# Loading tokens and weights of the first projection one k tile at a time, in a two-layer decoder trunk on Trainium2

## Chip, cores and metric

The kernel runs on one core of a Trainium2 chip. The metric is the device time of one execution in microseconds (us); the times shown are medians of several runs. The engines are TensorE (PE in the profile: matrix products; PEld is its weight load), VectorE (DVE), ScalarE (ACT), GpSimd (POOL) and SyncE (SP), which here issues every data transfer.

## What is computed

Two layers of a hybrid causal decoder run over 592 token columns: 16 learned meta tokens, 64 sample tokens (8 sequences of 8) and 512 prompt tokens, with a model width of 1024. Only the start of layer 0 matters here:

```python
xn = rms_norm(x, norm_mix[0])        # y = x * rsqrt(mean(x*x) + EPS) * gain
z  = xn @ w_in_ab[0]                 # q, k, v, o, input and forget gates; then q, k, v, gate
# heads 0..3: mLSTM, heads 4..7: retention; output projection; ConvFFN; layer 1 (HGRN2); ConvFFN; final norm
```

The norm's root is one number per token, so the kernel multiplies the tokens by the gain alone, projects them, and applies the root to the result of the projection. The sum of squares over the 1024 features is needed for that, but not for the products.

## The kernel before

Tokens lie with features on partitions, in eight k tiles of 128 features by 592 tokens (`x[0]` to `x[7]`). For float32 accuracy each operand of a product is split in two parts of a reduced format: a high part (a cast on ACT, line 295 for weights, line 215 for tokens) and a low part (what the cast lost, a subtraction on DVE, line 299 and line 216). Each product is then three: high by high, and the two mixed ones.

A block of the projection is one stretch of output columns. Block 0 and block 1 (`token_proj`) give the values of two mLSTM heads each, and four columns of gates: 260 output columns. Tokens are the stationary operand there, in five token tiles (one of 80 tokens, four of 128). Block 0 runs k by k over token tiles 0 to 3 at once, then does `norm_rows` (the sums of squares, `ssp`, by products with a column of 1/1024, then the root `rt` by small DVE operations), then tile 4. Block 1 runs tile by tile, and after tile 1 does `norm_bcast`, which spreads the root over partitions (`rb`). Block 2 is an action, `setup`, that loads constants. Then come the projections of q, k and so on (`proj`), eight k tiles of 128 columns each.

A block's weights are loaded by `raw_weights` into tiles `wr` (two buffers), each for four k tiles and 260 columns: one transfer of 256 columns (512 KB) and one of 4 columns (8 KB). `Split.make` turns one into `wh` and `wl` (three buffers each). A transfer into a `wr` buffer waits until the former one has been split. `stream` fetches the loads of two splits ahead of the running block.

`start` loads `x[0]` and the vectors, makes the gained tokens of k tile 0 (`gained`: `h` and `xl`) and its square (`norm_square`). Then block 0's weights are loaded, and `go_on` does the same for k tiles 1 to 7. Squares of tiles 1, 3 and 5 and their sum are made on POOL as a second partial sum, those of the others by ACT (square) and DVE (sum). Line 1600 adds the two partial sums; `norm_rows` makes products of both.

The row stream (`rows`, gates of the mLSTM heads) is interleaved later by the clock of products that the builder keeps. It writes into `mgr`, a tile that `setup` first fills with zeros: line 982 multiplies the constant tile `ca` by zero on POOL. All transfers go through SP in order.

The framework orders each engine's instructions when the program is built, by priority (program order) and by its own plan of what is ready; on the chip each engine then runs its list in order.

Of the kernel before, what the change touches and what calls it, by code (L numbers as in the profile page):

```python
# [9 lines left out]
F32 = mybir.dt.float32  # L10
F32R = mybir.dt.float32r
# [3 lines left out]
ALU = mybir.AluOpType  # L15
PSUM = bass.MemoryType.PSUM

D = 1024
# [5 lines left out]
NT = NMETA + NSAM + NP  # L24
# [13 lines left out]
V_NMIX, V_NFFN, V_NFIN, V_GNA, V_GNB, V_GNH, V_LB, V_CB, V_CW = 0, 16, 32, 40, 44, 48, 56, 72, 116  # L38
# [61 lines left out]
def trunk_kernel(ctx: ExitStack, tc: tile.TileContext, I, O):  # L100
    nc = tc.nc
    V, S, G, T = nc.vector, nc.scalar, nc.gpsimd, nc.tensor
    ld, st_q = nc.sync, nc.sync
# [3 lines left out]
    wp = ctx.enter_context(tc.tile_pool(name="wp", bufs=1))  # L107
# [54 lines left out]
    def tmp(name, n=NT, dt=F32):  # L162
        return tp.tile([128, n], dt, name=name, tag="t", bufs=4)
# [28 lines left out]
    vec = cp.tile([128, 248], F32, name="vec")  # L192
    gnh = cp.tile([128, 16], F32, name="gnh")
    csm = cp.tile([128, 165], F32, name="csm")
# [3 lines left out]
    ones = cp.tile([128, 128], F32R, name="ones")  # L198
    mean = cp.tile([128, 1], F32, name="mean")
# [4 lines left out]
    x = [None] * 8  # L204
    state = {"x": "xa", "h": "xb", "ssq": {}}

    def xslot(c, name, dt=F32):
        return ap.tile([128, NT], dt, name=f"{name}{c}", tag=f"{state[name]}{c}")

    def gained(c, gain):  # L210

        hi = xslot(c, "h", F32R)
        lo = ap.tile([128, NT], F32R, name=f"xl{c}", tag=f"xl{c}")
        g = vec[:, gain + c:gain + c + 1]
        S.activation(hi, x[c], AF.Copy, scale=g)
        V.scalar_tensor_tensor(out=lo, in0=x[c], scalar=g, in1=hi.bitcast(F32), op0=ALU.mult, op1=ALU.subtract)
        state[c] = (hi, lo)

    def norm_square(c, a=0, b=NT, eng=V, part=0):

        sq = tmp("sq" if part in state["ssq"] else "ssq")
        if eng is V:
            S.activation(sq[:, a:b], x[c][:, a:b], AF.Square)
        else:
            eng.tensor_tensor(out=sq[:, a:b], in0=x[c][:, a:b], in1=x[c][:, a:b], op=ALU.mult)
        if part not in state["ssq"]:
            state["ssq"][part] = sq
        else:
            acc = state["ssq"][part][:, a:b]
            eng.tensor_tensor(out=acc, in0=acc, in1=sq[:, a:b], op=ALU.add)  # L230
# [48 lines left out]


    class Split:
        def __init__(self, k, n, src, sums=None):
            self.k, self.n, self.src, self.sums, self.made = k, n, src, sums, None
            line.append(self)

        def sum_up(self):
# [4 lines left out]
        def make(self):  # L291
            self.sum_up()
            src = self.src() if callable(self.src) else self.src
            hi = wp.tile([128, self.k, self.n], F32R, name="wh", tag="wh", bufs=3)
            S.copy(hi, src)  # L295
            if line:
                line[0].sum_up()
            lo = wp.tile([128, self.k, self.n], F32R, name="wl", tag="wl", bufs=3)
            V.tensor_tensor(out=lo, in0=src, in1=hi.bitcast(F32), op=ALU.subtract)  # L299
            self.made = (hi, lo)  # L300
# [51 lines left out]
    def weights(*views):  # L352

        return [Split(r.shape[1], r.shape[2], r) for r in map(raw_weights, views)]

    def got(ws):
        return [sp.get() for sp in ws]
# [46 lines left out]
    def cols(w, c0, n=128):  # L404
        return w.rearrange("(k p) n -> p k n", p=128)[:, :, c0:c0 + n]
# [8 lines left out]
            post(p[:, off + first:off + NT])  # L414
        return (lambda: weights([cols(w, c0)]), body)

    def token_proj(w, pieces, emit, first=False, hook=None):

        n = sum(b for _, b in pieces)

        def load():
            return weights(*[[cols(w, c0, b)[:, k0:k0 + 4, :] for c0, b in pieces] for k0 in (0, 4)])

        def products(out, halves, k, t0, r):
            hi, lo = halves[k // 4]
            xh, xl = state[k]
            for i, (a, b) in enumerate(((xh, hi), (xh, lo), (xl, hi))):
                matmul(out, lhsT=a[:, t0:t0 + r], rhs=b[:, k % 4, :], start=(k == 0 and i == 0),
                       stop=(k == 7 and i == 2))

        def body(halves):
            p, halves = None, got(halves)
            if first:

                ps = [mm("tp"), mm("tp"), px("tq")]
                outs = [(t, r, ps[t // 2][:, 512 * (t % 2):512 * (t % 2) + 512]) for t, (t0, r) in enumerate(TILES)]
                for ts in ((0, 1, 2, 3), (4,)):
                    for k in range(8):
                        for t in ts:
                            t0, r = TILES[t]  # L440
                            products(outs[t][2][:r, 0:n], halves, k, t0, r)
                        yield
                    if ts[0] == 0:
                        norm_rows()
                for o in outs:
                    emit(*o)
                return
            for t, (t0, r) in enumerate(TILES):
                if hook is not None and t in (0, 1, 4):
                    p, o = px("tq"), 0  # L450
                else:
                    o = 512 * (t % 2)
                    p = mm("tp") if t % 2 == 0 else p
                for k in range(8):
                    products(p[:r, o:o + n], halves, k, t0, r)
                    yield
                emit(t, r, p[:, o:o + 512])
                if hook is not None and t == 1:
                    hook()
        return (load, body)  # L460
# [497 lines left out]
    def layer0():  # L958
        w = I["w_in_ab"][0]
        ca = ap.tile([128, 1776], F32, name="ca", tag="u1")  # L960
# [5 lines left out]
        mgr = ap.tile([36, 2, 5, 128], F32R, name="mgr", tag="u2")  # L966
# [8 lines left out]
        def setup():  # L975
            ld.dma_start(out=ca[:, 0:1600], in_=I["c_ab"])
            sel = tmp("sel", 512)[0:36, :]
            ld.dma_start(out=sel, in_=I["c_sel"])
            ld.dma_start(out=rm4, in_=I["c_rm"][0:4, :])
            ld.dma_start(out=gb, in_=I["gate0"])  # L980
            S.copy(selr, sel)
            G.tensor_scalar(out=mgr.rearrange("p a t i -> p (a t i)"), in0=ca[0:36, 0:1280], scalar1=0.0, scalar2=None,
                            op0=ALU.mult)
            for t in range(5):
                o = 4 * min(t, 1)
                G.tensor_copy(epst[:, :, t], epsr[:, o:o + 4])
            G.memset(tok3[64:128, 0, :, :], 1.0)
            V.tensor_scalar(out=gnh, in0=vec[:, V_GNA:V_GNA + 16], scalar1=0.5, scalar2=None, op0=ALU.mult)

        def emit_va(hp):  # L990
            f0 = emit_v(f"a{hp}")

            def f(t, r, p):
                f0(t, r, p)
                if t == 0:
                    if hp == 0:
                        G.memset(gt, 0.0)
                    G.memset(vs[f"a{hp}"][:, :, :, 128:129], 1.0)
                S.activation(gt[:r, t, 32 * hp:32 * hp + 4], p[:r, 256:260], AF.Copy, scale=state["rt"][:r, t:t + 1])
            return f  # L1000
# [222 lines left out]
        def mixer_b(h):  # L1223
# [54 lines left out]
            for t, (t0, r) in enumerate(TILES[1:]):  # L1278
# [10 lines left out]
        kb = lambda h: proj(w, 2568 + 128 * h, post_rot(h, 128 ** -0.5, "bl", "k"))  # L1289
        g_ = lambda h: proj(w, 3592 + 128 * h, silu_gate(("b", h)))  # L1290
        vb = lambda hp: token_proj(w, [(3080 + 256 * hp, 256)], emit_v(f"b{hp}"))
        blocks = [token_proj(w, [(1024, 256), (2048, 4)], emit_va(0), first=True),
                  token_proj(w, [(1280, 256), (2052, 4)], emit_va(1), hook=norm_bcast), action(setup),
                  q_(0), k_(0), q_(1), k_(1), o_(0), q_(2), k_(2), o_(1), q_(3), k_(3), o_(2), vb(0),
                  qb(0), kb(0), o_(3), qb(1), kb(1), g_(0), vb(1), qb(2), kb(2), g_(1), qb(3), kb(3), g_(2), g_(3)]
# [285 lines left out]

    xin = I["x0"].rearrange("p c n -> c p n")

    def start():
        for c in range(8):
            x[c] = xslot(c, "x")
        V.memset(ones.bitcast(F32), 1.0)
        V.memset(mean, 1.0 / D)
        ld.dma_start(out=x[0], in_=xin[0])
        ld.dma_start(out=vec, in_=I["vectors"])  # L1590
        gained(0, V_NMIX)
        norm_square(0)

    def go_on():
        for c in range(1, 8):
            ld.dma_start(out=x[c], in_=xin[c])
            gained(c, V_NMIX)
            norm_square(c, 0, NT, *((G, 1) if c in (1, 3, 5) else (V, 0)))
        both = state["ssq"]
        V.tensor_tensor(out=both[0], in0=both[0], in1=both.pop(1), op=ALU.add)  # L1600
        ld.dma_start(out=csm, in_=I["c_small"])


    SPANS = ((NMETA, TILES[3][0]), (TILES[3][0], NT))
# [29 lines left out]
                                       op1=ALU.mult)  # L1634
            ld.dma_start(out=O["y"][:, c:c + 2, a - NMETA:b - NMETA], in_=y)

    start()
    b0, s0, mix0 = layer0()
    b1, s1, mix1 = layer1()
    blocks = b0 + mix_proj(I["w_out_ab"][0], mix0, 0, V_NFFN, xin)  # L1640
# [2 lines left out]
    blocks.append(action(spill))  # L1643
    blocks += b1 + mix_proj(I["w_out_c"][0], mix1, 14, V_NFFN + 8, xd)
    blocks += ffn(1, None, SPANS)
    first = blocks[0][0]()
    go_on()
    blocks[0] = (lambda: first, blocks[0][1])
    interleave(stream(blocks), s0 + s1 + [finish(*sp) for sp in SPANS], 2)


# [57 lines left out]
```

## Time and profile before

| what | value |
|---|---|
| median of 3 runs | 1589.66 us (1588.35 to 1589.88) |
| profiled execution, its own time | 1593.28 us |
| its span, first to last instruction | 1591.4 us |
| mean granted PE clock in it | 0.989 of full speed |
| PE busy | 1537.6 us |
| DVE, ACT, POOL busy | 1153.5, 729.0, 208.3 us |

The profile is of one execution; times in it count from the span's start. A row of the timeline gives the start, the duration, the engine, the line, the operation and its tiles (out<-in), how many were merged, and in brackets how long the engine had been idle before and what ended that. A matmul's duration reaches into the next one's, so the distance of their starts is the pace. A window's row gives the busy time and the count of instructions of each engine, then the granted clock, the share of the DMA engines and GB/s. Granted clock 1.00 is 2.4 GHz and 0.50 is 1.2 GHz.

### The profile page before, as it was taken

How to read it: one execution, taken by the hardware profiler on the slowest of the kernel's cores; microseconds unless marked ns; L12 is line 12 of the kernel's file. 1: busy time of each engine (PE TensorE's matmuls, PEld its weight loads, DVE VectorE, ACT ScalarE, POOL GpSimd, SP SyncE). 2: the span in 40 equal slices, each digit the busy share in tenths (PEclk: the TensorE clock that was granted, in tenths of full speed). 3: DMA queues.
4: the chain of work that ended last, by engine and by line, in shares of the span. 5: the costliest groups of instructions: out<-in, count | busy, mean ns of one | idle time of the engine just before them, and what ended most of it. 6: DMA issues, size and time to landing. Idle time of an engine off the chain costs nothing. (4 is left out here: it accounts for less than half of the span.)

```text
span 1591.4 us, 32114 instructions
## 1 busy us (share of the span) xinstructions
PE 1537.6 (97%) x13100; PEld 1489.0 (94%) x13100; DVE 1153.5 (72%) x2351; ACT 729.0 (46%) x1316; POOL 208.3 (13%) x402
## 2 busy tenths in 40 slices
PE   5999999999999999999999899999999999999996
PEld 5999998999999999999999798998999999999995
DVE  6576564658987887777646776766689888788875
ACT  3543343325454444444445566464454444444453
POOL 4000000000120001011003524333002000000001
PEclk9999999999999999999999999999999999999998
DMA  6555646233223323223522231223332232333234
GB/s 165 102 81 113 86 90 78 80 123 107 80 67 96 91 80 94 80 82 119 159 80 59 65 96 65 88 91 104 93 103 80 80 94 82 92 93 94 67 108 130
DMA packets 217620, 148.57 MB, mean 93 GB/s; under 512 B 7512, under 2 KB 208984, under 8 KB 217472
## 3 DMA queue, kind: packets, MB, share of 16 engines
q1 hardware_dynamic: 217472, 146.51, 34.4%
q8 instruction: 103, 1.69, 0.4%
q14 instruction: 45, 0.37, 0.1%
HBM read 131.84 MB, written 14.65 MB: 92 GB/s over the span
## 5 line engine op out<-in xcount | busy, mean ns | idle before, releaser
L295 ACT CAST wh<-wr 128x1024 fp32r<-128x1024 f32 (+3 forms) x240 | 232.7, 970 | 403.2 <-PE dp L123 121.6
L299 DVE TENSOR_TENSOR wl<-wr,wh 128x1024 fp32r<-128x1024 f32 (+3 forms) x240 | 271.4, 1131 | 75.8 <-ACT wh L295 73.8
L123 PE MATMUL dp<-h,wh 128*128 128x296 f32 (+1 forms) x1088 | 242.3, 304 | 0.7 <-ACT v_c L918 0.5
L123 PE MATMUL dp<-h,wl 128*128 128x296 f32 (+1 forms) x1088 | 236.7, 298 | 0.0
L123 PE MATMUL dp<-xl,wh 128*128 128x296 f32 (+1 forms) x1088 | 236.6, 298 | 0.0
L123 PE MATMUL dp<-bh,wh 128*128 128x296 f32 (+2 forms) x864 | 188.4, 299 | 0.8 <-DVE x L491 0.4
L123 PE MATMUL dp<-bh,wl 128*128 128x296 f32 (+2 forms) x864 | 186.4, 297 | 0.0
L123 PE MATMUL dp<-bl,wh 128*128 128x296 f32 (+2 forms) x864 | 186.4, 297 | 0.0
L123 PEld LDWEIGHTS dp<-h,wh 128*128 128x128 f32 x1088 | 174.9, 189 | 4.3 <-issue 1.8
L123 PEld LDWEIGHTS dp<-h,wl 128*128 128x128 f32 x1088 | 176.4, 189 | 0.0
L123 PEld LDWEIGHTS dp<-xl,wh 128*128 128x128 f32 x1088 | 176.2, 189 | 0.0
L123 PEld LDWEIGHTS dp<-bh,wh 128*128 128x128 f32 x864 | 139.0, 188 | 3.1 <-issue 1.4
L123 PEld LDWEIGHTS dp<-bl,wh 128*128 128x128 f32 x864 | 139.5, 188 | 0.0
L123 PEld LDWEIGHTS dp<-bh,wl 128*128 128x128 f32 x864 | 139.2, 188 | 0.0
L123 PE MATMUL ac<-h,wh 128*128 128x296 f32 (+1 forms) x408 | 123.8, 303 | 3.0 <-DVE cs L704 2.7
L123 PE MATMUL ac<-h,wl 128*128 128x296 f32 (+1 forms) x408 | 121.5, 298 | 0.0
L123 PE MATMUL ac<-xl,wh 128*128 128x296 f32 (+1 forms) x408 | 121.1, 297 | 0.0
L123 PE MATMUL tp<-wh,h 128*128 128x256 f32 (+3 forms) x280 | 85.1, 305 | 14.8 <-ACT wh L295 11.2
L595 ACT ACTIVATE cv<-cv 128x612 f32<-128x612 f32 (+1 forms) x44 | 31.1, 708 | 117.0 <-DVE cv L591 117.0
L295 ACT CAST wh<-s 128x1024 fp32r<-128x1024 f32 x68 | 56.8, 836 | 60.7 <-PE sb L123 34.6
L123 PEld LDWEIGHTS ac<-h,wh 128*128 128x128 f32 x408 | 76.9, 188 | 6.9 <-DVE cs L704 5.6
L123 PE MATMUL tp<-wl,h 128*128 128x256 f32 (+3 forms) x280 | 81.7, 292 | 0.3 <-DVE wl L299 0.3
(477 smaller groups left out, 3455.9 us busy)
## 6 DMA issues: line engine op xcount, KB each, us to landing
wr<-in_w_ffn_in SPq DMA_DIRECT2D x88, 512.0 KB, 3.8
wr<-in_w_in_ab SPq DMA_DIRECT2D x32, 512.0 KB, 7.6
wr<-in_w_ffn_out SPq DMA_DIRECT2D x32, 512.0 KB, 3.4
wr<-in_w_in_c SPq DMA_DIRECT2D x32, 512.0 KB, 3.9
wr<-in_w_ffn_out SPq DMA_DIRECT2D x24, 384.0 KB, 3.5
x<-in_x SPq DMA_DIRECT2D x16, 296.0 KB, 5.2
out_H<-s_s SPq DMA_DIRECT2D x8, 576.0 KB, 2.8
wr<-in_w_out_ab SPq DMA_DIRECT2D x16, 256.0 KB, 2.7
```

What stands on the lines that cost most here:

```text
L123: T.matmul(out, lhsT=lhsT, rhs=rhs, **kw)
L295: S.copy(hi, src)
L299: V.tensor_tensor(out=lo, in0=src, in1=hi.bitcast(F32), op=ALU.subtract)
L595: S.activation(env_["cv"][:, b0:612], env_["cv"][:, b0:612], AF.Silu)
```

## The change

`start` becomes a function of the k tile, which the first block's load calls for each of the eight in turn. It loads `x[k]`, then the weights of that k tile (one transfer of 256 columns, 128 KB, and one of 4 columns, 2 KB), and then emits the gain and the square of that tile. The vectors are loaded ahead of `x[0]`, and the small constants `csm` after the last k tile, as before. The weights are split one k tile at a time (`single`): eight casts and eight subtractions of 260 columns in place of two and two of 1040. All squares are made on ACT and all sums on DVE, in one partial sum, so the merge at line 1600 and five of ten `ssp` products go. `mgr` is filled in three pieces of up to 512 columns from `rb` in place of one of 1280 from `ca`.

```diff
     class Split:
-        def __init__(self, k, n, src, sums=None):
+        def __init__(self, k, n, src, sums=None, single=False):
...
             hi = wp.tile([128, self.k, self.n], F32R, name="wh", tag="wh", bufs=3)
+            if self.single:
+                lo = wp.tile([128, self.k, self.n], F32R, name="wl", tag="wl", bufs=3)
+                for k in range(self.k):
+                    S.copy(hi[:, k, :], src[:, k, :])
+                    V.tensor_tensor(out=lo[:, k, :], in0=src[:, k, :], in1=hi[:, k, :].bitcast(F32), op=ALU.subtract)
+                self.made = (hi, lo)
+                return
...
         def load():
+            if chunks is not None:
+                raws = [wp.tile([128, 4, n], F32, name="wr", tag="wr", bufs=2) for _ in range(2)]
+
+                def one(k):
+                    o = 0
+                    for c0, b in pieces:
+                        ld.dma_start(out=raws[k // 4][:, k % 4, o:o + b], in_=cols(w, c0, b)[:, k, :])
+                        o += b
+
+                for k in range(8):
+                    chunks(k, one)
+                return [Split(4, n, r, single=True) for r in raws]
...
-            G.tensor_scalar(out=mgr.rearrange("p a t i -> p (a t i)"), in0=ca[0:36, 0:1280], scalar1=0.0, scalar2=None,
-                            op0=ALU.mult)
+            for a in range(0, 1280, 512):
+                b = min(a + 512, 1280)
+                G.tensor_scalar(out=mgr.rearrange("p a t i -> p (a t i)")[:, a:b], in0=state["rb"][0:36, 0:b - a],
+                                scalar1=0.0, scalar2=None, op0=ALU.mult)
...
-        blocks = [token_proj(w, [(1024, 256), (2048, 4)], emit_va(0), first=True),
+        blocks = [token_proj(w, [(1024, 256), (2048, 4)], emit_va(0), first=True, chunks=start),
...
-    def start():
-        for c in range(8):
-            x[c] = xslot(c, "x")
-        V.memset(ones.bitcast(F32), 1.0)
-        V.memset(mean, 1.0 / D)
-        ld.dma_start(out=x[0], in_=xin[0])
-        ld.dma_start(out=vec, in_=I["vectors"])
-        gained(0, V_NMIX)
-        norm_square(0)
-
-    def go_on():
-        for c in range(1, 8):
-            ld.dma_start(out=x[c], in_=xin[c])
-            gained(c, V_NMIX)
-            norm_square(c, 0, NT, *((G, 1) if c in (1, 3, 5) else (V, 0)))
-        both = state["ssq"]
-        V.tensor_tensor(out=both[0], in0=both[0], in1=both.pop(1), op=ALU.add)
-        ld.dma_start(out=csm, in_=I["c_small"])
+    def start(c, load):
+
+        if c == 0:
+            V.memset(ones.bitcast(F32), 1.0)
+            V.memset(mean, 1.0 / D)
+            ld.dma_start(out=vec, in_=I["vectors"])
+        x[c] = xslot(c, "x")
+        ld.dma_start(out=x[c], in_=xin[c])
+        load(c)
+        gained(c, V_NMIX)
+        norm_square(c)
+        if c == 7:
+            ld.dma_start(out=csm, in_=I["c_small"])
...
-    start()
...
-    first = blocks[0][0]()
-    go_on()
-    blocks[0] = (lambda: first, blocks[0][1])
```

## Rows read from the trace of the kernel before

**Rows 1.** The page, engine totals over the whole span.

```profile
PE 1537.6 (97%) x13100; PEld 1489.0 (94%) x13100; DVE 1153.5 (72%) x2351; ACT 729.0 (46%) x1316; POOL 208.3 (13%) x402
```

**Rows 2.** Windows: stretch, length, busy time of each engine, clock, DMA share, GB/s.

```profile
1.65:14.10 12.45, 2.52 (x10) 2.22 (x11) 3.59 (x13) 2.90 (x5) 0.07 (x1) 1.00 0.78 186
...
34.20:40.10 5.90, 5.85 (x28) 5.86 (x29) 2.55 (x11) 1.06 (x1) 0.00 (x0) 0.50 0.63 142
40.20:55.40 15.20, 15.20 (x127) 15.10 (x126) 5.98 (x18) 10.48 (x31) 0.00 (x0) 1.00 0.61 112
...
200.00:1550.00 1350.00, 1329.25 (x11552) 1290.95 (x11551) 1003.03 (x1918) 628.37 (x1106) 181.81 (x369) 0.99 0.31 90
...
272.30:279.10 6.80, 5.70 (x34) 4.83 (x34) 2.61 (x6) 2.64 (x8) 0.00 (x0) 0.50 1.00 53
```

**Rows 3.** Timeline of PE in the first 43 us.

```profile
11.25 0.72 PE L123 MATMUL tp<-wh,h 128*80 128x260 f32 x2 [11.25 <-ACT wh L295]
...
34.25 2.13 PE L123 MATMUL ssp<-mean,ssq 128*80 128x1 f32 x10 [3.17 <-DVE ssq L1600]
...
36.60 0.42 PE L123 MATMUL tq<-wh,xl 128*128 128x260 f32 x1
36.82 0.42 PE L123 MATMUL tq<-wh,h 128*128 128x260 f32 x1
...
41.92 0.28 PE L123 MATMUL tq<-wh,h 128*80 128x260 f32 x1
```

**Rows 4.** Timeline of DVE in the first 43 us.

```profile
28.04 0.82 DVE L216 SCALAR_TENSOR_TENSOR xl<-x,vec,h 128x592 fp32r<-128x592 f32 x1
28.79 0.77 DVE L230 TENSOR_TENSOR ssq<-ssq,sq 128x592 f32<-128x592 f32 x1
29.48 1.23 DVE L299 TENSOR_TENSOR wl<-wr,wh 128x1040 fp32r<-128x1040 f32 x1
30.63 3.57 DVE L1600 TENSOR_TENSOR ssq<-ssq 128x592 f32<-128x592 f32 x1
```

**Rows 5.** Timeline of POOL in the first 43 us.

```profile
25.26 3.66 POOL L986 COPY epst<-csm 128x4 f32<-128x4 f32 x5
29.86 4.15 POOL L982 TENSOR_SCALAR mgr<-ca 36x1280 fp32r<-36x1280 f32 x1 [0.95 <-DMA ca<-in_c_ab]
```

**Rows 6.** Timeline of ACT in the first 43 us.

```profile
4.34 0.77 ACT L215 ACTIVATE h<-x,vec 128x592 fp32r<-128x592 f32 x1
...
14.18 1.06 ACT L295 CAST wh<-wr 128x1040 fp32r<-128x1040 f32 x1 [2.99 <-DMA wr<-in_w_in_ab]
...
20.29 0.70 ACT L223 ACTIVATE sq<-x 128x592 f32<-128x592 f32 x1 [1.74 <-POOL ssq L230]
```

**Rows 7.** Transfers issued at 0.74, 2.12, 11.75, 17.32, 17.73 us: KB, us to landing.

```profile
x<-in_x SPq DMA_DIRECT2D x1, 296.0 KB, 3.0
...
wr<-in_w_in_ab SPq DMA_DIRECT2D x1, 8.0 KB, 7.9
...
x<-in_x SPq DMA_DIRECT2D x1, 296.0 KB, 7.0
...
wr<-in_w_in_ab SPq DMA_DIRECT2D x1, 512.0 KB, 5.4
...
wr<-in_w_in_ab SPq DMA_DIRECT2D x1, 8.0 KB, 10.1
```

**Rows 8.** Timeline of SP around 12 us.

```profile
11.75 0.65 SPq L1596 DMA_DIRECT2D x<-in_x  x1
```

**Rows 9.** What SP waited for in the first 35 us: total, times, longest.

```profile
SPq L348 <- DVE wl L299: 10.1, 2, 9.2
...
SPq L1601 <- DMA wr<-in_w_in_ab: 1.0, 1, 1.0
```

**Rows 10.** Timeline of PE around 273 us.

```profile
273.40 0.43 PE L127 MATMUL p<-csm,bl 128*80 128x128 f32 x1 [3.19 <-DVE bl L1122]
```

**Rows 11.** What PE waited for from 60 to 1550 us: total, times, longest.

```profile
PE p L127 <- DVE bl L1122: 3.7, 4, 3.2
```

More of the change, by code (lines that the diff above doesn't have):

```diff
@@ L281, in trunk_kernel @@
     class Split:
-        def __init__(self, k, n, src, sums=None):
-            self.k, self.n, self.src, self.sums, self.made = k, n, src, sums, None
+        def __init__(self, k, n, src, sums=None, single=False):
+            self.k, self.n, self.src, self.sums, self.single, self.made = k, n, src, sums, single, None
             line.append(self)
@@ L415, in proj, with token_proj @@
         return (lambda: weights([cols(w, c0)]), body)
-    def token_proj(w, pieces, emit, first=False, hook=None):
+    def token_proj(w, pieces, emit, first=False, hook=None, chunks=None):
         n = sum(b for _, b in pieces)
         def load():
+            if chunks is not None:
[8 more added lines that the diff above has]
+                return [Split(4, n, r, single=True) for r in raws]
             return weights(*[[cols(w, c0, b)[:, k0:k0 + 4, :] for c0, b in pieces] for k0 in (0, 4)])
```

## Prediction

> **What bounds the kernel now.** I read the page's engine totals first: the matmul engine (TensorE, PE) is busy for 1537.6 of 1591.4 us [rows 1], so 54 us of the span are its idle time, and only those, and the time in which it runs at half clock, can be won. Then the windows: from 200 to 1550 us it is busy for 1329 of 1350 us, with the DMA engines at 0.31 [rows 2]. Work late in the kernel is thus paced by PE, not by a transfer stream that began at time zero, and a shift at the beginning should reach the end one for one. The change touches the first 42 us, so I read those engine by engine.
>
> PE's first product starts at 11.25 us, released by the cast of the first half of the weights [rows 3]. It then works through block 0 (96 products of token tiles 0 to 3, 24 of tile 4), stands still for 3.17 us before the sums of squares (ssp), goes on at half clock (0.50 from 34.2 to 40.1 us [rows 2]; two products start 0.22 us apart [rows 3], against 15.2 us for 127, 0.12 each, from 40.2 to 55.4 at full clock [rows 2]), and reaches k tile 4 of block 1 at 41.92 us [rows 3]. That moment, call it M, is my yardstick: what follows it is the same work in both kernels.
>
> The ssp wait ends on the merge of the two partial sums at line 1600. It takes 3.57 us, while an addition of that shape at 28.79 takes 0.77 [rows 4]; GpSimd's (POOL's) fill of mgr runs beside it from 29.86 for 4.15 us [rows 5]. ACT's squares wait for POOL's additions too: 1.74 us at 20.29, as one example of two [rows 6].
>
> **The change part by part.**
>
> *Squares on ACT and DVE only.* It removes three POOL squares and two POOL additions, one merge (3.57 us before ssp), and five of the ten ssp products (2.13 us for ten [rows 3], so about 1.07). It adds three ACT squares (0.70 each) and two DVE additions net of the merge (0.77 each). Per k tile ACT then does gain 0.77, square 0.70 and one weight cast; DVE does the low part 0.82, an addition 0.77 and one low part of weights. The two small weight operations (128x260) have no row; I bound each by a quarter of the 1040-column rows (1.06/4 = 0.27, 1.23/4 = 0.31) and half of them (0.53, 0.62), and take 0.4. Per k tile: ACT 1.9, DVE 2.0 us [rows 4, 6].
>
> *Transfers in order of use.* Before, both weight halves stood ahead of tokens 1 to 7. Now each k tile is one token transfer (296 KB), one weight piece (128 KB) and one of 2 KB. Bytes are the same: tokens 2.42 MB, weights 1.06, vectors 0.13. In the mixed stretch 1.65 to 14.1 us they came at 186 GB/s [rows 2]; the seventh token transfer, issued at 11.75 [rows 8], took 7.0 us [rows 7], so landed at 18.8, with one more behind it. I keep this sum of bytes and take 19 us for the last k tile, 2.0 us apart; bounds 17.5 and 25.4 (rival 2). Issues on SP become 26 in place of 14, at about 0.45 us some 12 us, below 19. The first k tile: the first transfer of before took 3.0 us from its issue [rows 7]; the small piece is issued by about 2.5, so lands near 5.5 (up to 10 if it takes 7.9, as a small piece did [rows 7]); cast and low part make the first product start near 6.0 in place of 11.25.
>
> The Trainium skill (DMA: Bandwidth & Descriptors, section Bandwidth) speaks against this part: it asks for DMAs of 1 MiB and more and gives some 2.0 us fixed for each. The 24 pieces one after the other would be an estimated 56 us by that page; the rows show transfers overlapping, so I don't follow it in the sum, but rival 2 stands beside it.
>
> *PE through block 0.* From 6.0 PE is first paced by the clock, then by arrivals. Low edge: the last k tile lands at 19, plus 0.77, 0.82, fifteen products of 0.12 and ssp 1.1: 23.5. High edge: all 120 products at 0.217 from 6.0 plus ssp: 33.1. I take 24, since DVE's 2.0 us per k tile and the arrivals both allow it; k tile 4 of block 1 could start 12 products later, at 25.4.
>
> *What is late next.* Block 1's second weight half goes into the buffer that block 0's second half leaves, so its transfer waits on SP for the low part of the last k tile. Before, SP waited for low parts of weights twice by 35 us, 10.1 us in all [rows 9]. Now the last low part of block 0 is made at 19 + 2.5 = 21.5, the 2.5 being gain, low part and addition in a row (0.77 + 0.82 + 0.77) and what of the small split shows. Behind it on SP stand ca, the weights of q 0, sel, the gate rows and a state tile: they move too, but are wanted only after block 1. From the issue at 22: landing after 5.4 us (its large part of before) to 10.1 us (its small part [rows 7]); then 1.06 cast and 1.23 low part [rows 4, 6]. M lies at 29.8 to 34.5; I take 32. So the stall moves: PE, which stood at ssp, will stand before k tile 4 of block 1.
>
> *Sum.* 41.92 - 32 = 9.9 us. While PE waits it can do tile 1's first 12 products, +1.4. The wait (26.9 to 32) is longer than the 3.17 us after which the granted clock was 0.50, so I charge 18 products x 0.097 = 1.75 us. Net 9.6 us.
>
> *mgr from the norm's broadcast.* Before it waited for ca; now for rb, available after ssp, the root and the broadcast. Three fills, 4.15 us together as bound from above, end near 40 us. Their reader, the row stream, runs after block 1, so they cost nothing; without that cover at most 4.15. The DVE operations beside them can take up to 3.57 in place of 0.77, as the merge did; those I find there (rotary tables times rb) have no PE reader until much later. The root's chain of small operations starts after ssp and hides behind tiles 0 and 1 of block 1, as before.
>
> *Rest.* Fewer ssp products shift the builder's clock by the same amount for all later streams. But engines don't run in program order (POOL copies epst, line 986, before it fills mgr, line 982 [rows 5]): a planner orders each queue at build time, so later order may move a little. I put that at 0, with bounds of -6 and +6 (rival 4).
>
> Against the profiled execution: span 1591.4 - 9.6 = 1581.8, with the 1.9 around it 1583.7. That execution (1593.28) is 3.6 above the median of the runs, 1589.66, so I forecast the median at **1580**.
>
> **The rivals.**
>
> 1. *Splits behind squares.* Gains and squares stand ahead of the small splits in program order. If the planner thinks ACT or DVE full, PE's first product waits until all squares are done, near 20.5. Then 120 x 0.12 + 1.75 + 1.1 gives 37.8, M = 39.2: gain 2.7, 1587. For: DVE has 2.0 us of work per 2.0 us of arrivals. Against: before, ACT took the second weight cast at 14.18, ahead of the square at 20.29 [rows 6], which stands earlier in the program. 12%.
>
> 2. *Latency in place of bytes.* The fourteenth transfer, csm at line 1601, waited for a weight transfer [rows 9], the sixth at the latest: eight seem to be in flight at most. 24 transfers in three rounds of 7.9 us [rows 7] end at 25.4; last low part 27.9, M 36.1 to 40.8, middle 38.5: gain 3.4 + 1.4 - 1.75 = 3.1, 1586.6. Against: 7.9 was measured behind much larger transfers. 10%.
>
> 3. *No new stall.* Block 1's half lands as fast as its large part did, and PE has filler: M near 27, gain 15, 1574.7. 20%.
>
> 4. *Slower: the later order.* At 273.40 PE stands 3.19 us for the transposes of one retention head, and the clock is at 0.50 to 279.1 [rows 2, 10]: 5.70 us busy there would be 2.9 at full clock, so 6.0 in all. Four heads have this wait, together 3.7 us [rows 11], so only one is long. If the new plan makes the other three long, the sum is -9.6 + 18 = +8.4: 1598. It decides from two on (+2.4, 1592). Against: the dense stream is untouched there. 6%. One gone would give 1574.
>
> 5. *Not k by k.* If a split waited for the whole half tile, the first product would start near 12.5 and block 0 end near 31.8; M 33.2, 1581.5. Inside the forecast's range, 5% within its share.
>
> **How the numbers follow.** Forecast 52%, 1575 to 1585 (M 29.8 to 34.5, clock charge or not, one later stall off). Rivals 12, 10, 20 and 6%. For 8 in 10 the range goes from 1573 to 1588, which takes in rivals 1 to 3. About 0.2%, 3.2 us, is what a measurement of this kernel can tell from no change: forecast and rival 3 are faster (72%), rivals 1 and 2 fall on both sides of that line (8% faster, 14% within), rival 4 slower: 0.80, 0.14, 0.06.
>
> **What would show it.** First product near 6 us, one cast of weights after each square on ACT, low parts of 0.82 on DVE with no 2 us ones, no idle time before ssp, five ssp products, mgr after rb, and a PE wait of some 5 us before k tile 4 of block 1, ended by the cast of weights. Wrong: PE starting near 20 (rival 1), tokens landing after 23 (rival 2), no wait in block 1 (rival 3), or new waits after 100 us (rival 4).

## The result and the profile after

| | before | after |
|---|---|---|
| median of 4 runs each | 1589.01 us (1588.31 to 1589.88) | 1580.57 us (1577.87 to 1582.41) |
| profiled execution, its own time | 1593.28 us | 1579.73 us |
| its span | 1591.4 us | 1578.0 us |

The medians differ by 8.4 us. The ratio of the runs is 0.9937, with a 95% interval from 0.9918 to 0.9957. The two profiled spans differ by more, 13.4 us, because the profiled execution of before is 4.3 us above its median. To see which part belongs to the change, I matched the n-th product on PE in both traces (both have 13100; I count from 0, so the 300th has 300 ahead of it). The 300th starts at 61.68 us before and at 53.41 after, 8.26 earlier. The 700th is 8.27 earlier and the 1500th 8.34. So the beginning gives 8.3 us, which is the difference of the medians, and the other 5 us come in steps late in the kernel, the largest from 9.8 at the 7500th product to 12.8 at the 7900th. Between 900 and 1000 us the mean granted clock was 0.97 in before's execution and 1.00 in after's, where the code is the same. Both traces have the same wait of PE there, 0.55 us at 967.79 before and 0.56 at 957.97 after; behind it the clock stood at 0.50 for 6.8 us in before's execution, and at 1.00 in after's. So I don't count this step for the change; the smaller ones were not followed up.

The engine totals of the page of after, beside [rows 1]:

```profile
PE 1530.4 (97%) x13100; PEld 1483.8 (94%) x13100; DVE 1148.9 (73%) x2359; ACT 730.9 (46%) x1325; POOL 194.2 (12%) x399
```

The timeline of PE in after, beside [rows 3]:

```profile
6.05 0.72 PE L123 MATMUL tp<-wh,h 128*80 128x260 f32 x2 [6.05 <-ACT wh L298]
...
16.36 0.40 PE L123 MATMUL tp<-wh,h 128*80 128x260 f32 x2
...
18.28 0.40 PE L123 MATMUL tp<-wh,h 128*80 128x260 f32 x2
...
20.57 1.13 PE L123 MATMUL ssp<-mean,ssq 128*80 128x1 f32 x10
...
23.46 0.28 PE L123 MATMUL tq<-wh,xl 128*128 128x260 f32 x1
24.68 0.47 PE L123 MATMUL tq<-wh,h 128*80 128x260 f32 x2 [0.94 <-ACT wh L302]
25.72 0.39 PE L123 MATMUL tp<-wh,h 128*128 128x260 f32 x1 [0.57 <-ACT gtd L1021]
...
30.85 0.40 PE L123 MATMUL tq<-wh,h 128*80 128x260 f32 x2
...
40.86 0.58 PE L123 MATMUL tp<-wh,h 128*128 128x260 f32 x1 [3.64 <-ACT gtd L1021]
```

The first product starts at 6.05 in place of 11.25. From k tile 3 on, a k tile takes PE 1.92 us (16.36 to 18.28), which is sixteen products of 0.12: twelve of token tiles 0 to 3 and four of tile 4, which PE takes in between. PE paces itself there. The ssp wait of 3.17 us is gone, and k tile 4 of block 1 starts at 30.85 without a wait. The new row is the last one: 3.64 us of idle time before token tile 3 of block 1, ended by a copy on ACT.

The timelines of ACT, DVE and POOL in after follow. ACT first, one k tile of block 0 and then block 1:

```profile
14.66 0.79 ACT L215 ACTIVATE h<-x,vec 128x592 fp32r<-128x592 f32 x1
15.35 0.69 ACT L223 ACTIVATE sq<-x 128x592 f32<-128x592 f32 x1
15.94 0.39 ACT L298 CAST wh<-wr 128x260 fp32r<-128x260 f32 x1
16.24 0.79 ACT L215 ACTIVATE h<-x,vec 128x592 fp32r<-128x592 f32 x1
...
23.57 1.06 ACT L302 CAST wh<-wr 128x1040 fp32r<-128x1040 f32 x1 [5.66 <-DMA wr<-in_w_in_ab]
...
27.55 1.06 ACT L302 CAST wh<-wr 128x1040 fp32r<-128x1040 f32 x1 [0.34 <-DMA wr<-in_w_in_ab]
...
35.66 1.05 ACT L302 CAST wh<-wr 128x1024 fp32r<-128x1024 f32 x1 [3.96 <-DMA wr<-in_w_in_ab]
36.61 0.62 ACT L1001 CAST selr<-sel 36x512 fp32r<-36x512 f32 x1
...
37.73 0.46 ACT L938 ACTIVATE v_a<-tq,rt 80x256 f32<-80x256 f32 x1
...
40.20 0.47 ACT L938 ACTIVATE v_a<-tp,rt 128x256 f32<-128x256 f32 x1
40.55 0.26 ACT L1021 ACTIVATE gtd<-tp,rt 128x4 f32<-128x4 f32 x1
```

DVE:

```profile
16.44 0.83 DVE L216 SCALAR_TENSOR_TENSOR xl<-x,vec,h 128x592 fp32r<-128x592 f32 x1
17.18 0.77 DVE L230 TENSOR_TENSOR ssq<-ssq,sq 128x592 f32<-128x592 f32 x1
17.87 0.42 DVE L299 TENSOR_TENSOR wl<-wr,wh 128x260 fp32r<-128x260 f32 x1
18.21 0.82 DVE L216 SCALAR_TENSOR_TENSOR xl<-x,vec,h 128x592 fp32r<-128x592 f32 x1
...
19.64 0.42 DVE L299 TENSOR_TENSOR wl<-wr,wh 128x260 fp32r<-128x260 f32 x1
...
28.64 1.24 DVE L306 TENSOR_TENSOR wl<-wr,wh 128x1040 fp32r<-128x1040 f32 x1
...
32.16 1.18 DVE L1029 TENSOR_TENSOR ca<-ca,rb 128x592 f32<-128x592 f32 x1
```

POOL:

```profile
31.22 3.83 POOL L1004 TENSOR_SCALAR mgr<-rb 36x256 fp32r<-36x256 f32 x3 [10.70 <-ACT rb L274]
```

The last row of PE and the rows of ACT from 35.66 on belong together. ACT stands 3.96 us, until the weights of q 0 have landed, and casts them. Then it casts `sel`. Only behind these two in its list stand the copies of block 1's values out of TensorE's output tiles, token tiles 0, 1 and 2 at 37.73, 39.11 and 40.20, although tile 0's last product had started at 33.24. Tile 3's products go into the other half of the output tile `tp` that tile 2 fills, and they start only when tile 2's copies are done (40.55 + 0.26 = 40.81; PE goes on at 40.86). An output tile of its own for tile 3 might remove the wait too; no run tried it.

Transfers of after, beside [rows 7]: KB and us from issue to landing. The first two were issued at 11.62 and 12.09 (the last k tile), the next at 14.44 (block 1's first half, its small part), 14.86 (`ca`), 20.09 (block 1's second half) and 25.93 (the weights of q 0).

```profile
x<-in_x SPq DMA_DIRECT2D x1, 296.0 KB, 4.0
wr<-in_w_in_ab SPq DMA_DIRECT2D x1, 128.0 KB, 3.9
...
wr<-in_w_in_ab SPq DMA_DIRECT2D x1, 8.0 KB, 9.1
...
ca<-in_c_ab SPq DMA_DIRECT2D x1, 800.0 KB, 10.6
...
wr<-in_w_in_ab SPq DMA_DIRECT2D x1, 512.0 KB, 6.8
...
wr<-in_w_in_ab SPq DMA_DIRECT2D x1, 512.0 KB, 9.7
```

The last k tile's tokens and 128 KB of weights are there at 12.09 + 3.9 = 16.0; its 2 KB piece, issued at 12.94, has no landing in the trace, and its cast comes at 17.52. The windows of after (stretch, length, busy time of PE, PEld, DVE, ACT and POOL, clock, DMA share, GB/s):

```profile
26.80:30.20 3.40, 3.40 (x18) 3.40 (x17) 2.94 (x7) 1.47 (x3) 0.00 (x0) 0.50 0.67 85
...
40.50:43.80 3.30, 2.94 (x13) 2.94 (x14) 0.00 (x0) 0.31 (x2) 0.00 (x0) 0.50 1.04 76
```

At the start PE's products stand 0.22 us apart, until 9.5 us. After that the first 60 us have two short stretches at half clock (1.2 GHz), each after waits of PE: 0.94 and 0.57 us ahead of the first, 3.64 ahead of the second.

### The profile page after: what moved, and what is told of

Same layout as the page of the kernel before. It is cut to its first block, busy times and chain, and to the rows that moved or that the text cites. A ratio compares the mean times of both kernels' runs of the same rounds, so it can differ in the third digit from the quotient of the medians.

```text
span 1578.0 us, 32152 instructions
## 1 busy us (share of the span) xinstructions
PE 1530.4 (97%) x13100; PEld 1483.8 (94%) x13100; DVE 1148.9 (73%) x2359; ACT 730.9 (46%) x1325; POOL 194.2 (12%) x399
## 5 line engine op out<-in xcount | busy, mean ns | idle before, releaser
L306 DVE TENSOR_TENSOR wl<-wr,wh 128x1024 fp32r<-128x1024 f32 (+3 forms) x238 | 267.9, 1126 | 75.4 <-ACT wh L302 73.2
L123 PE MATMUL tp<-wh,h 128*128 128x256 f32 (+3 forms) x280 | 82.8, 300 | 12.8 <-ACT wh L298 6.0
L123 PE MATMUL sb<-b2h,wl 128*128 128x296 f32 (+1 forms) x272 | 81.0, 298 | 0.0
```

Of the source, the lines that this page charges most:

```text
L123: T.matmul(out, lhsT=lhsT, rhs=rhs, **kw)
```

## Experiments

The theory after the first look: the gain at the beginning is 13.2 us (the 160th product starts at 44.06 before and at 30.85 after), and 5 of it are given back around the start of token tile 3 of block 1, where the copies of values stand in ACT's list behind a cast that waits for a late transfer. The rivals: that squares alone or loads alone make the gain, that the fill of `mgr` takes part in it, and that the transfer of `ca` (800 KB) is what makes the others late. Where a median of before is given, it is from the same chip as the kernel beside it.

**Squares alone.** Before, with all squares on ACT and sums on DVE.

```diff
-            norm_square(c, 0, NT, *((G, 1) if c in (1, 3, 5) else (V, 0)))
-        both = state["ssq"]
-        V.tensor_tensor(out=both[0], in0=both[0], in1=both.pop(1), op=ALU.add)
+            norm_square(c)
```

> Squares part alone: the kernel before with all squares on ACT and all sums on DVE, loads and splits as before, mgr from ca. Theory (both parts gain on their own, each through a wait that another part still bounds): the wait of 3.17 us before ssp goes, five ssp products (1.1 us) go, the half clock after the wait (1.75 us) goes or shrinks; PE still starts at 11.25 us. 4 to 6 us below the kernel before, near 1584. Rival (the squares matter only once the loads come early): the last token lands at the same time, so ssp waits for the tokens and the gain is under 2 us, 1587 or more.

Measured: 1585.04 us against 1591.18, ratio 0.9966 (0.9947 to 0.9985). In the trace the 100th product is 6.21 us earlier than in before, the 300th 4.71. (Its first product, at 9.97, was 1.28 us earlier although the loads are the same: the first half of the weights was cast at 8.86 in place of 10.14. The second half, behind which the tokens are made, was cast at 14.45 against 14.18, so this isn't part of the gain.) Its PE and DVE:

```profile
34.99 0.35 PE L123 MATMUL tq<-wl,h 128*80 128x260 f32 x1 [1.77 <-DVE wl L299]
```

```profile
30.25 0.17 DVE L187 TENSOR_TENSOR rs_a<-rt 128x5 f32<-128x5 f32 x1
30.45 2.90 DVE L188 SCALAR_TENSOR_TENSOR rs_a<-rs_a,ms 128x5 f32<-128x5 f32 x1
```

The ssp wait has gone, so the squares alone carry about 4.7 us. The merge was not the only operation that POOL's part had lengthened: a low part of weights took 2.02 us at 15.27 in before, beside a square on POOL, and 1.24 at 15.54 here. Some of the 6.2 is given back in block 1. There DVE, in its list, has the root's small operations ahead of a low part of weights, and one of them takes 2.90 us where its neighbours take 0.17. POOL's fill of `mgr` from `ca` runs from 30.33 for 3.44 us beside it. This is the same collision as the slow merge in before [rows 4, 5], now on the root.

**Loads alone.** After, with squares and the merge as in before.

```diff
-        norm_square(c)
+        norm_square(c, 0, NT, *((G, 1) if c in (1, 3, 5) else (V, 0)))
         if c == 7:
+            both = state["ssq"]
+            V.tensor_tensor(out=both[0], in0=both[0], in1=both.pop(1), op=ALU.add)
```

> The changed kernel with the squares of k tiles 1, 3 and 5 back on POOL and the merge back on DVE. Theory: POOL needs some 9 us for three squares and two sums and slows DVE beside it (2.0 us low parts), so the last low part of weights comes some 3 to 5 us later than at 20.1, block 1's second half lands later by the same, and some 3 to 5 us of the gain go: 1583 to 1586. Rival (with the early loads the squares have slack, ssp being off the path): no change against the changed kernel, 1580 to 1581.

Measured: 1586.42 us, ratio 0.9967 (0.9954 to 0.9981). The 100th product is 11.44 us earlier than in before, the 160th 12.40, the 200th only 3.54, and the 300th 3.51. PE and the DVE merge:

```profile
39.95 0.86 PE L123 MATMUL dp<-h,wh 128*128 128x296 f32 x2 [6.11 <-ACT wh L302]
```

```profile
22.31 0.76 DVE L1619 TENSOR_TENSOR ssq<-ssq 128x592 f32<-128x592 f32 x1
```

The size came near the expected one (0.4 us above its range). The place didn't: what loads win is lost in one wait of 6.11 us for weights, which land late, and in the half clock around it (37.7 to 44.5 us). The merge itself took 0.76 us here, since POOL's fill was elsewhere; so the 3.57 of [rows 4] was the price of the fill beside it. The early gains of the two parts, 4.71 and 3.51, add up to 8.2, near the 8.26 of both, but neither is a clean share: each ended at another wait.

**The fill of `mgr`.** After, with `mgr` filled from `ca` again.

```diff
-            for a in range(0, 1280, 512):
...
+            G.tensor_scalar(out=mgr.rearrange("p a t i -> p (a t i)"), in0=ca[0:36, 0:1280], scalar1=0.0, scalar2=None,
+                            op0=ALU.mult)
```

> The changed kernel with mgr filled from ca again. ca lands at 25.5 us there, so the fill would run on POOL from 25.5 to some 29.6, beside DVE's diagonal tiles and the low part of block 1's second weight half (24.2 to 29.9). Theory: this is no part of the path by itself, but DVE beside POOL is slowed as the merge was (3.57 for 0.77), so k tile 4 of block 1 comes 1 to 3 us later: 1581 to 1584. Rival (POOL slows DVE only with operands of the full width): the same as the changed kernel within 1.5 us.

Measured: 1580.11 us, ratio 0.9931 (0.9912 to 0.995), so the same as after (0.9937). DVE:

```profile
25.95 3.04 DVE L270 SCALAR_TENSOR_TENSOR dg<-csm,rt,dg 128x80 fp32r<-128x80 f32 x1
```

The collision comes back: an operation of 0.30 us in after (at 25.82) takes 3.04 beside POOL's fill (from 25.17 for 4.17 us), and PE waits 0.61 and 0.16 us for its successors. But the 300th product is only 0.45 us later than in after. This execution kept full clock from 26.8 to 30.2, where after's had 0.50, so the fairer neighbour is the second run of after (below), which kept it too: against that one the 160th product is 2.50 us later and the 300th 0.57. PE has the wait before token tile 3 ahead of it anyway (3.10 us here, 5.35 there), and that one swallows most of the delay.

**The first cast behind the values.** After, with q 0's cast put behind the copy of tile 2's values in ACT's list. The diff of what matters:

```diff
-            S.copy(hi, src)
+            cast = S.copy(hi, src)
+            if "behind" in state:
+                tc.add_manual_dep(cast.ins, state.pop("behind").ins.name, order_dep, reason="values first")
...
-            pump()
+            if not getattr(body, "late", False):
+                pump()
...
+                if hook is not None and t == 2:
+                    state["behind"] = state["value"]
+                    pump()
```

> The changed kernel with one order added: ACT's cast of q 0's weights stands behind the value copies of block 1's token tile 2 in ACT's list. Theory (PE's wait of 3.64 us at 40.86 us is ACT standing 3.96 us for q 0's weights, which land at 35.6, with the values of block 1 behind it): the wait goes, and with it the half clock from 40.4 to 43.9 (some 1.5 us): 4 to 5.5 us below the changed kernel, 1575 to 1577. Rival (the values are late by their own chain, root and broadcast, or PE waits for something else): PE still waits 2 us or more before token tile 3 of block 1, and the time is 1579 to 1581.

Measured: 1580.57 us, ratio 0.9935 (0.9917 to 0.9952), no different from after. PE and ACT:

```profile
39.57 0.58 PE L123 MATMUL tp<-wh,h 128*128 128x260 f32 x1 [4.07 <-ACT gtd L1028]
```

```profile
35.90 0.62 ACT L1008 CAST selr<-sel 36x512 fp32r<-36x512 f32 x1 [5.34 <-DMA sel<-in_c_sel]
...
38.90 0.47 ACT L945 ACTIVATE v_a<-tp,rt 128x256 f32<-128x256 f32 x1
...
39.41 1.05 ACT L302 CAST wh<-wr 128x1024 fp32r<-128x1024 f32 x1
```

The expected gain did not come. The cast of weights moved behind the values (39.41), and the next thing ahead of them, the cast of `sel`, waited 5.34 us for its own transfer. That doesn't yet tell a wait at the head of ACT's list from some other cause before tile 3.

**Both casts behind the values.** The same, with the cast of `sel` moved too (`state["third"]` is the same copy as `state["behind"]`).

```diff
-            S.copy(selr, sel)
+            c_ = S.copy(selr, sel)
+            tc.add_manual_dep(c_.ins, state["third"].ins.name, order_dep, reason="values first")
```

> The changed kernel with both casts that wait for late transfers (q 0's weights and the selector rows, sel) put behind the value copies of block 1's token tile 2 in ACT's list. In the run with only the first of them moved, ACT stood 5.34 us for sel instead, and PE 4.07 us. Theory (ACT's list, in order, holds the values behind whatever transfer is late): nothing late stands ahead of the values now, the PE wait is under 0.5 us, the 300th product starts at 48 to 49.5 us, 4 to 5.5 us below the changed kernel. Rival (the values are bound by PE's slots or by the root's chain): PE still waits 2 us or more, and the time stays.

Beside it on the same chip, after once more:

> The changed kernel once more, so that the next three stand beside it on one chip. Both theories: 8 to 9 us below the kernel before; PE waits 3.6 us before token tile 3 of block 1, its 300th product starts at 53.4 us.

Measured: 1576.33 us (1574.61 to 1579.97) for both casts moved, ratio to before 0.9908 (0.9886 to 0.993); after again 1581.56 us, ratio 0.9941 (0.9922 to 0.996). ACT and a window of the former:

```profile
35.23 0.48 ACT L945 ACTIVATE v_a<-tp,rt 128x256 f32<-128x256 f32 x1 [1.04 <-PE tp L123]
...
36.34 1.05 ACT L302 CAST wh<-wr 128x1024 fp32r<-128x1024 f32 x1 [0.47 <-DMA wr<-in_w_in_ab]
```

```profile
26.00:41.00 15.00, 14.98 (x122) 14.75 (x123) 7.22 (x16) 10.45 (x28) 3.83 (x3) 1.00 0.71 153
```

Now the values wait for PE, not PE for them. PE is busy for 14.98 of 15 us from 26 to 41, at full clock, and the 300th product starts at 47.15, 6.3 us earlier than in after. By the 700th, 3.8 are left: PE then waits 1.1 us for ACT (at 49.35) and 0.9 for DVE (at 57.00) in the projections. The medians differ by 5.2 us; the intervals of the two ratios overlap a little (0.9922 to 0.993). This shows the cause: the wait before token tile 3 is that of ACT's list for late transfers, and removing it is worth 3.8 us in these traces and 5.2 in the medians. This version is the fastest that I ran.

After again, PE's wait, with what ended ACT's:

```profile
40.62 0.58 PE L123 MATMUL tp<-wh,h 128*128 128x260 f32 x1 [5.35 <-ACT gtd L1021]
```

```profile
35.42 1.04 ACT L302 CAST wh<-wr 128x1024 fp32r<-128x1024 f32 x1 [5.67 <-DMA wr<-in_w_in_ab]
```

This execution had full clock from 9.7 to 40.4, so PE reached tile 3 earlier and waited 5.35 us in place of 3.64; its 300th product started at 53.29, against 53.41. The landing of q 0's weights (cast at 35.42 and 35.66) sets the time, and whatever PE wins ahead of it is lost in the wait.

**`ca` held back.** After, with the load of `ca` made to wait for the norm's root.

```diff
         def setup():
+            V.tensor_copy(ca[:, 0:1], state["rt"][:, 0:1])
             ld.dma_start(out=ca[:, 0:1600], in_=I["c_ab"])
```

> The changed kernel with the load of ca held back until the norm's root is there (one column is copied into ca ahead of it), so that ca no longer shares the queue with block 1's weights. Theory (block 1's first half lands at 23.5 because ca's 800 KB run beside it): it lands at 19 to 21, PE's waits of 0.94 and 0.57 us before 26 us go, and q 0's weights, 9.7 us on their way before, land some 3 us or more sooner; but q 0's cast now stands ahead of rb in ACT's list, so PE still waits 1 to 3 us: 1577 to 1579. Rival (the 16-byte pieces of the gate columns, not ca, make the landing late): landing at 23 as before, no gain, 1580 to 1582.

Measured: 1584.49 us, ratio 0.9957 (0.994 to 0.9975). The median is 2.9 us above that of after on the same chip; the intervals overlap. The expected 1577 to 1579 did not come. Transfers, block 1's second half and q 0's weights, then ACT and PE:

```profile
wr<-in_w_in_ab SPq DMA_DIRECT2D x1, 512.0 KB, 4.1
...
wr<-in_w_in_ab SPq DMA_DIRECT2D x1, 512.0 KB, 11.4
```

```profile
20.19 1.06 ACT L302 CAST wh<-wr 128x1040 fp32r<-128x1040 f32 x1 [1.87 <-DMA wr<-in_w_in_ab]
...
36.71 1.04 ACT L302 CAST wh<-wr 128x1024 fp32r<-128x1024 f32 x1 [7.28 <-DMA wr<-in_w_in_ab]
```

```profile
37.81 0.86 PE L123 MATMUL dp<-h,wh 128*128 128x296 f32 x2 [7.08 <-ACT wh L302]
```

Half of the theory held. Without `ca` beside them, block 1's first half was cast 3.4 us earlier (20.19 against 23.57) and its second half landed after 4.1 us in place of 6.8. But the bytes of `ca` then travel beside q 0's weights, which take 11.4 us in place of 9.7, and PE stands 7.08 us for them. At the 700th product this trace is 2.3 us behind after's.

The profiled execution is the slowest of the ten (1589.39), and by the 1500th product it has lost another 7.4 us to after, in one more wait and the half clock around it (0.50 from 123.7 to 130.5):

```profile
125.58 0.41 PE L127 MATMUL p<-csm,bl 128*80 128x128 f32 x1 [5.89 <-DVE zq L839]
```

DVE stood there behind a split of weights for which ACT had waited 13.45 us (cast at 122.73); a state tile issued beside those weights took 18.1 us, against 12.7 in after. Whether the other nine executions have this wait is not known, so the 2.9 us are no clean price of the held-back `ca`.

**Cast behind the values, and `ca` held back.** Both edits at once, the cast of `sel` not moved.

> The changed kernel with q 0's cast behind the values and ca held back until the root. Theory: sel is issued ahead of ca there and lands by 22, so ACT has nothing late ahead of the values: PE waits under 1 us before token tile 3, block 1's halves land 2 to 4 us sooner, the half clock at 27 and at 40 us goes, the 300th product starts at 46 to 48.5 us: 5 to 8 us below the changed kernel. Rival (something else of the row stream, which needs ca times rb, comes late in its place): the 300th product at 50 us or later.

Measured: 1581.75 us, ratio 0.9942 (0.9922 to 0.9963), the same as after; the expected 5 to 8 us did not come. The wait before token tile 3 is gone (`sel`, issued ahead of `ca` here, is cast at 21.21, so nothing late stands ahead of the values) and the 300th product starts at 49.83, 3.6 us earlier than in after, but by the 700th the lead over before is 7.82, less than after's 8.27. ACT:

```profile
41.25 1.05 ACT L302 CAST wh<-wr 128x1024 fp32r<-128x1024 f32 x1 [2.23 <-DMA wr<-in_w_in_ab]
...
50.67 1.04 ACT L302 CAST wh<-wr 128x1024 fp32r<-128x1024 f32 x1 [7.85 <-DMA wr<-in_w_in_ab]
```

The next two projections' weights are late in their turn. Moving `ca` moves the lateness down the stream; it doesn't remove it.

## Why the prediction was right, and where it was not

The time (1580 forecast, 1580.57 measured) and the moment M (32 forecast, 30.85 measured) came out. The way to M and the way from M to the end did not.

*First product.* 6.0 forecast, 6.05 measured.

*Work per k tile.* The small splits were put at 0.4 and took 0.39 (ACT) and 0.42 (DVE). The sums of durations, 1.9 and 2.0, are right too (0.79 + 0.69 + 0.39 and 0.83 + 0.77 + 0.42), but operations overlap at their edges: one k tile follows the next after 1.58 us on ACT (14.66 to 16.24) and 1.77 on DVE (16.44 to 18.21). PE, at 1.92, was the slowest of the three, so it paced the end of block 0. The forecast had arrivals and DVE as the pace.

*Transfers.* Forecast 19 for the last k tile, measured 16.0. The row of 7.0 us [rows 7] came from a stream with two weight halves ahead of it; the transfers here took 4.0 and 3.9. Rival 2 (7.9 us in rounds of eight) is refuted by the same rows. So is the estimate of 56 us that the prediction made from the Trainium skill (DMA: Bandwidth & Descriptors): the advice on size stands in its section Bandwidth, but the fixed 2.0 us stand in its section Anatomy of one DMA, as a fit for transfers issued from GpSimd, while these go through SP. The trace doesn't agree with 56 us: small transfers that overlap did not pay their fixed costs one after the other here, and the last tokens with their 128 KB of weights were there at 16.0.

*ssp.* The wait went, as forecast. That five of ten products go, as the section on the change says too, was wrong: the row says x10 in both kernels, and PE has 13100 in both. Before had already merged its two partial sums at line 1600, so the products were made of one. The row shrank from 2.13 to 1.13 us because the clock was 1.00 in place of 0.50, so the size of the term (1.07) was met by accident.

*Block 0's end and block 1's second half.* Forecast 24 for the end, measured 23.46 for its last product's start. Last low part of block 0: forecast 21.5, measured 19.64 + 0.42 = 20.1. From the issue (20.09, forecast 22), the transfer took 6.8 us, inside the forecast 5.4 to 10.1; cast and low part followed as costed and were done at 28.61 and 29.88. But M, at 30.85, was not set by that chain. PE came to k tile 4 without a wait, and late because its own products before it ran partly at half clock; in the second run of after, at full clock, the same k tile starts at 28.89. That M lay within 1.15 us of the forecast was luck.

*"PE will stand some 5 us before k tile 4 of block 1."* This was wrong. PE stood 0.94 and 0.57 us earlier, for block 1's first half and for a copy, and then had filler up to k tile 4. The first half is a step that the prediction did not price: it landed at 23.5, 9.1 us after its issue, with `ca` issued right behind it. In the run with `ca` held back it landed 5.3 us after its issue.

*The yardstick.* Against the 160th product (13.2 us earlier) the forecast of 9.6 net was low by 3.6: M earlier by 1.15, filler worth 2.1 (13.2 less the 11.1 at M) in place of 1.4, and the 1.75 for half clock, which did occur (26.8 to 30.2) but inside M. Then "what follows M is the same work" failed. Of the 13.2, 5.0 were given back at token tile 3, by 3.64 of waiting before it and by about 13 products at 0.22 in place of 0.12 in it. The prediction named q 0's weights and `sel` among the transfers behind block 1's second half, and dismissed them as wanted only after block 1. That holds for PE, their last reader. It does not hold for ACT, their first, whose list has their casts ahead of block 1's copies. Two errors in opposite directions, 3.6 and 5.0 us, gave a net of 8.3 for the 9.6 forecast. The 1580 was thus right partly because they cancelled.

*mgr costs nothing.* Held: the run that undoes it is the same as after. That it also gains nothing follows from the wait that covers it. The DVE operation beside its pieces takes 1.18 us at 32.16, where its neighbour takes 0.81, not the 3.57 given as a bound.

*The rivals.* Rival 1 happened only within each k tile: a cast stands behind that tile's square, which puts at most the square's 0.7 us ahead of PE's first product, not all squares. Rival 3 (no new stall, 1574.7) is not what the change did, but it is what the version with both casts moved comes near: 1576.33. Rival 4 did not come: the lead stays at 8.3 from the 300th to the 1500th product, and the one long wait for a retention head is there as before (3.25 us at 265.05). Rival 5 did not come either: the first product needed only its own k tile.

*What stays open.* Why q 0's weights take 9.7 us in after, while block 1's half took 4.1 in one run. It isn't `ca`, which had landed at 25.5 (14.86 + 10.6), before their issue at 25.93. `sel`, the gate rows and a state tile of 516 KB, issued between 26.34 and 29.57, and the next 512 KB of weights, issued at 30.78, travel beside them and were not taken away singly. Nor are the 2.5 us that the best version gives back between the 300th and the 700th product, against before, taken apart beyond its two waits.

## What to carry over

When a stall is removed at the beginning, look for the next late transfer by its first reader, not by the engine that needs the result: a small cast on an in-order engine holds everything that stands behind it in the list. Count the gain at several later points, since 13 us at one point were 8 some 10 us later. An operation moved out of the way of one late transfer can uncover the next, so move all of them before judging the idea: one moved cast gave nothing, two gave 5 us in the medians.

## What the hardware showed unexpectedly

- The first DVE operation to begin while POOL's fill of 1280 columns ran ended only about when the fill did, within 0.42 us of its end in the trace, whatever its own size: 3.57 us for 0.77 [rows 4, 5], 2.90 for 0.17 and 3.04 for 0.30. The low part of weights at 29.48, begun before the fill, took its usual 1.23 [rows 4, 5]. Beside the fill in pieces of up to 512 columns an operation took 1.18 (32.16 in after), where the same one took 0.77 in the run with `mgr` filled from `ca`. The pieces also read `rb` in place of `ca`; no run takes the two apart.
- A transfer of 512 KB in the first 60 us took from 4.1 us (block 1's second half, `ca` held back) to 11.8 us (q 0's weights, both edits at once) from issue to landing.
- In after the granted clock fell to 0.50 at 26.8 us, following waits of 0.94 and 0.57 us (ending at 24.68 and 25.72). The second run of after, with waits of 0.27 and 0.93 us there, and the version with both casts moved, with one of 1.16 us at 25.95, kept 1.00.
